# Q/k slabs as Strassen pairs, and all seven SSM projection products inside the attention stage

## The chip, the cores and the metric

The kernel runs on one core of a Trainium2 chip. The metric is device microseconds of one execution; lower is better. TensorE (PE) does the matmuls, VectorE (DVE) and ScalarE (ACT) the elementwise work, GpSimd (POOL) some masking and scaling, and SyncE (SP) issues every DMA transfer, in the order in which they stand in its program. Each of these engines works through its own list of instructions in order.

## The reference

One layer of a hybrid decoder, sequence 1024, width 1024, batch 1. A Mamba-2 (SSD) branch and an attention branch with a forget gate read the same modulated, normalised input `h`.

```python
proj = einsum("bsd,de->bse", h, w_in)                 # z, xbc, dt, q, k, v, z_att, f, gates
y_ssm = _ssd_branch(z_ssm, xbc, dt_raw, ...)          # conv, chunked state space, gated RMS norm
y_att = _fox_branch(q, k, v, z_att, f_logit, b_f)     # 8 heads of 128, causal softmax with decay
g_ssm, g_att = split(sigmoid(g_logit + b_gate), 2)
merged = g_ssm * (y_ssm @ w_proj_ssm) + g_att * (y_att @ w_proj_att)
x = x + gate * (merged @ w_out)
return _rmsnorm(x, final_norm_w)
```

Everything is float32. The kernel reaches that precision on PE by splitting each operand into a high and a low part (`split`: a CAST on ACT, a subtraction on DVE) and taking three products: high·high, high·low, low·high.

## The kernel before

The work stands in stages, one after the other in the program; a list scheduler then fixes the order on each engine, by priorities and by its own model of durations. Work that is written inside `tc.high_priority` goes first; the rest fills in where its inputs are there.

- **Input and first slabs** (to about 76 us): the modulated `h`, transposed and split, as `hh` and `hl` (8 tiles each).
- **Projection stage** (pool `pa`, to about 492 us): the columns of `w_in` are worked off as slabs of 128 output columns. `c_slab` is a plain slab: two halves of 8 x 3 matmuls of 512 columns, 48 in all. `c_pair` makes two slabs at once with Strassen's seven products (Winograd's form): 7 x 4 x 3 = 84 matmuls in place of 96, with four extra sums of weights on DVE. `PAIRS` lists the pairs, 19 of them. `w_sums`, spread over the pairs by `WPREP`, prepares the same kind of sums for the later projections.
- **State-space stage** (pool `sd`, to about 729 us): `ssd_half`, at high priority. Plain slabs fill PE beside it: three v slabs and the seven q/k slabs of `SPILL`, by the table `FILL`. A spilled slab is written to DRAM (`qk_out`).
- **Attention stage** (pools `at`, `atp`, to about 1018 us): `attend(h)` for eight heads at high priority: logits (tile `lg`), min and exp (`sm`, `pr`), scaling by POOL, transposes (`tp`), split (`pth`, `ptl`), and the product with v (`pv`). The next head's q and k come from `qk_slab`: loaded and split where they were spilled, or made on the spot by `c_slab`. `u_scaled` scales the state-space result (tile `ut`) with `rb`, a row that comes from the end of the state-space stage through DRAM, and writes `us_scr`; `PREP` says after which heads. `early` makes the SSM projection's products 1 and 2 after head 6 and product 6 after head 7. A product of a projection is four column blocks of 12 matmuls, 48 in all.
- **Last stage** (pools `frp`, `finp`): SSM products 7, 5, 4, 3, then the seven products of the attention projection (inputs `o_scr`, loaded as `b11`, `b21`, `b12`, `b22`; products 1 and 2 need `b11` and `b21`), then the seven of the output projection. Pool `frp`, which holds `b11`, `b21` and the merge tiles `m`, lies where the attention stage's pool `at` lay. `b12` and `b22` lie in pool `fin`.

The tiles `ev` (four buffers of 1024 columns) are shared by `ut`, `qt`, `vt`, `zg`, `gt` and others. DMA transfers run on eight lanes; a transfer waits for the one before it on its lane.

Of the kernel before, what the change touches and what calls it, by code (L numbers as in the profile page):

```python
# [65 lines left out]
def build(ctx, tc, t):  # L66
# [866 lines left out]
    def early(js):  # L933
# [6 lines left out]
        def form(i):  # L940
            fs = []
            for k in range(4):
                if i == 2:
                    e = piece(4 + k, LO)
                else:
                    e = piece(k, LO)
                    for q in {1: (), 6: (12, 22)}[i]:
# [10 lines left out]
        if js == (6,):  # L958
            for p in range(4):
                hi, lo = w_in("ps", 6, p)  # L960
                ps = bank()
                for k in range(4):
                    c = slice(k * P, (k + 1) * P)
                    PE.matmul(ps, lhsT=hi[:, c], rhs=fs[6][k][0], start=(k == 0), stop=False)
                    PE.matmul(ps, lhsT=hi[:, c], rhs=fs[6][k][1], start=False, stop=False)
                    PE.matmul(ps, lhsT=lo[:, c], rhs=fs[6][k][0], start=False, stop=(k == 3))
                V.tensor_tensor(out=sx[p], in0=ps, in1=sx[p], op=ALU.add)
            return
        for p in range(4):
            mine = {}  # L970
            for i in js:
                prod_c(i, "ps", fs[i], sx, mine, done, p)

    with tc.tile_pool(name="at", bufs=1, side="right") as at, \
            tc.tile_pool(name="atp", bufs=1, space=PSUM) as atp:

        def qk_slab(h):
            qh, ql, kh, kl = (at.tile([P, S], F32R, tag=n, bufs=2, name=n) for n in ("qh", "ql", "kh", "kl"))
            def q_evac(hs, ps):
                A.activation(out=qh[:, hs], in_=ps, func=AF.Copy, scale=-QSCALE)  # L980
                V.scalar_tensor_tensor(out=ql[:, hs], in0=ps, scalar=-QSCALE, in1=f32(qh[:, hs]),
                                       op0=ALU.mult, op1=ALU.subtract)

            def k_evac(hs, ps):
                A.copy(out=kh[:, hs], in_=ps)
                V.tensor_tensor(out=kl[:, hs], in0=ps, in1=f32(kh[:, hs]), op=ALU.subtract)
            for n, slab, evac, hi, lo in (("q", Q0 + h, q_evac, qh, ql), ("k", K0 + h, k_evac, kh, kl)):
# [84 lines left out]
        for h in range(AH):  # L1072
            if h == HCLOSE:
                hctx.close()
                fin = finx.enter_context(tc.tile_pool(name="fin", bufs=1))
# [19 lines left out]
    with tc.tile_pool(name="finp", bufs=1, space=PSUM) as fpp_:  # L1095
        fpp.append(fpp_)


        done_early = sum(EARLY.values(), ())
        b = {**ub, **b_quads(us_scr, (11, 21))}  # L1100
        def ssm_done(ch, tk, p, ps):
            V.scalar_tensor_tensor(out=mq[11 + 10 * ch + tk][p], in0=g_in(p + 4 * ch, tk), scalar=1.0, in1=ps,
                                   op0=ALU.add, op1=ALU.mult)
        prep_u = True
        for i in ORDER:
# [144 lines left out]
```

## Time and profile before

| | us |
|---|---|
| median of 3 runs (lowest, highest) | 1225.61 (1225.07, 1229.4) |
| the profiled execution, its own time | 1224.89 |
| span of the profile, first to last instruction | 1223.2 |
| PE, DVE, ACT, POOL busy | 1162.6, 957.2, 626.5, 88.3 |

Busy time of PE is the union of pipelined matmuls, so a PE that is always busy may still be fed too slowly; the count of matmuls in a stretch tells more. A page of the profile gives the busy time of each engine in a stretch with the number of instructions behind it (x304 is 304 instructions).

### The profile page before, as it was taken

The numbers are of one execution on the slowest core, as the hardware profiler recorded it, in microseconds if no ns is written. First come the engines' busy times: TensorE is split into PE (matmuls) and PEld (weight loads), VectorE is DVE, ScalarE is ACT, GpSimd is POOL, SyncE is SP. The second block draws the span as 40 slices with busy tenths as digits, with TensorE's granted clock in tenths as the row PEclk, the third lists the DMA queues.
The fourth block names the chain that finished last, engine by engine and source line by source line (L and its number), as shares of the span: only waits on it lengthen the run. The fifth ranks groups of instructions, "written<-read, shape, count | busy, mean of one in ns | idle before, by whom it ended". The sixth has DMA issues, their size and how long they took to land.

```text
span 1223.2 us, 18391 instructions
## 1 busy us (share of the span) xinstructions
PE 1162.6 (95%) x6206; PEld 976.3 (80%) x6206; DVE 957.2 (78%) x1950; ACT 626.5 (51%) x1252; POOL 88.3 (7%) x152
## 2 busy tenths in 40 slices
PE   4899999999999999999999989999989998999997
PEld 2788888788877878998987777888877886788876
DVE  6956689788987685589999986664677968989967
ACT  5554444453443334777676633454456644354465
POOL 2000000000000000000000002222322220000001
PEclk9899999999999999999999999999999999999999
DMA  8765543655485665646545658422255526965333
GB/s 351 274 233 184 185 154 93 231 189 189 129 309 167 224 224 200 202 152 223 187 150 186 199 213 294 155 92 73 87 176 195 182 77 239 326 190 182 104 96 147
DMA packets 109018, 228.26 MB, mean 187 GB/s; under 512 B 12362, under 2 KB 20220, under 8 KB 107900
## 3 DMA queue, kind: packets, MB, share of 16 engines
q1 hardware_dynamic: 108924, 227.09, 55.1%
q8 instruction: 49, 0.80, 0.3%
q14 instruction: 45, 0.37, 0.1%
HBM read 159.14 MB, written 67.90 MB: 186 GB/s over the span
## 4 chain that ended last, share of the span: by engine, by line
PE 66%; DVE 15%; DMA 12%; issue 4%; ACT 3%; POOL 1%; SPq 0%; DVEq 0%; POOLq 0%; ACTq 0%
PE pp L497 4%; PE pp L499 4%; PE pp L500 4%; PE pv L1061 4%; PE mm L497 3%; PE mm L499 3%; PE mm L112 3%; PE mm L500 3%; PE mm L113 3%; PE lg L1030 3%; PE mm L111 3%; DMA ab<-a_scr 3%; PE tp L1051 2%; PE mm L915 2%; PE mm L913 2%
## 5 line engine op out<-in xcount | busy, mean ns | idle before, releaser
L98 ACT CAST wh<-wr 128x512 fp32r<-128x512 f32 (+1 forms) x214 | 130.8, 619 | 171.7 <-DMA wr<-w_c 35.0
L99 DVE TENSOR_TENSOR wl<-wr,wh 128x512 fp32r<-128x512 f32 (+1 forms) x214 | 145.5, 686 | 44.9 <-ACT wh L98 44.6
L112 PE MATMUL mm<-hl,wh 128*128 128x512 f32 x288 | 116.4, 404 | 1.9 <-DVE hl L306 1.9
L111 PE MATMUL mm<-hh,wh 128*128 128x512 f32 x288 | 115.7, 406 | 0.1
L113 PE MATMUL mm<-hh,wl 128*128 128x512 f32 x288 | 115.1, 400 | 0.0
L136 PE MATMUL mm<-wh,hh 128*128 128x256 f32 (+1 forms) x256 | 73.8, 289 | 2.4 <-DVE tmp L348 2.4
L137 PE MATMUL mm<-wl,hh 128*128 128x256 f32 (+1 forms) x256 | 74.4, 292 | 0.0
L138 PE MATMUL mm<-wh,hl 128*128 128x256 f32 (+1 forms) x256 | 73.6, 288 | 0.0
L1036 ACT ACTIVATE pr<-pr,sm 128x1024 f32<-128x1024 f32 (+3 forms) x64 | 49.9, 780 | 44.8 <-DVE sm L1035 38.1
L1054 ACT CAST pth<-tp 128x512 fp32r<-128x512 f32 (+1 forms) x80 | 42.5, 542 | 53.5 <-PE tp L1051 43.7
L1031 DVE CUSTOM_DVE_ANT_0 pr<-lg,fb 128x512 f32<-128x512 f32 (+1 forms) x96 | 51.3, 551 | 18.7 <-PE lg L1030 13.2
L112 PEld LDWEIGHTS mm<-hl,wh 128*128 128x128 f32 x288 | 55.0, 191 | 13.2 <-DVE hl L306 3.3
L113 PEld LDWEIGHTS mm<-hh,wl 128*128 128x128 f32 x288 | 54.9, 191 | 10.3
L111 PEld LDWEIGHTS mm<-hh,wh 128*128 128x128 f32 x288 | 54.5, 191 | 10.5 <-ACT hh L305 0.7
L690 ACT ACTIVATE ab<-ab,acs 128x128 f32<-128x128 f32 x128 | 41.2, 391 | 37.7 <-DMA ab<-a_scr 34.1
L1055 DVE TENSOR_TENSOR ptl<-tp,pth 128x512 fp32r<-128x512 f32 (+1 forms) x80 | 49.9, 630 | 10.2 <-ACT pth L1054 9.8
L1039 POOL TENSOR_SCALAR pr<-pr,sm 128x1024 f32<-128x1024 f32 (+3 forms) x64 | 52.2, 816 | 78.2 <-DVE sm L1038 65.4
L98 ACT CAST sh<-sr 128x512 fp32r<-128x512 f32 x57 | 33.9, 619 | 42.3 <-DVE sr L479 31.3
L796 POOL TENSOR_TENSOR fl<-fl,mhalf 128x8 f32<-128x8 f32 x1 | 1.6, 1648 | 699.0 <-DVE fl L794 699.0
L136 PEld LDWEIGHTS mm<-wh,hh 128*128 128x128 f32 x256 | 48.8, 191 | 2.8 <-DVE tmp L348 2.6
L138 PEld LDWEIGHTS mm<-wh,hl 128*128 128x128 f32 x256 | 49.1, 192 | 0.0
L137 PEld LDWEIGHTS mm<-wl,hh 128*128 128x128 f32 x256 | 48.9, 191 | 0.2
(406 smaller groups left out, 3485.5 us busy)
## 6 DMA issues: line engine op xcount, KB each, us to landing
wr<-w_c SPq DMA_DIRECT2D x116, 256.0 KB, 3.7
wa<-w_ada SPq DMA_DIRECT2D x8, 1024.0 KB, 11.4
g_scr<-gt SPq DMA_DIRECT2D x16, 512.0 KB, 4.2
ab<-a_scr SPq DMA_DIRECT2D x32, 256.0 KB, 3.9
gt<-g_scr SPq DMA_DIRECT2D x32, 256.0 KB, 4.0
wr<-w_ps SPq DMA_DIRECT2D x28, 256.0 KB, 2.7
wr<-w_pa SPq DMA_DIRECT2D x28, 256.0 KB, 2.7
wr<-so SPq DMA_DIRECT2D x28, 256.0 KB, 2.7
```

Source lines behind the costliest of these rows:

```text
L98: A.copy(out=hi[:, :n], in_=raw[:, :n])
L99: eng.tensor_tensor(out=lo[:, :n], in0=raw[:, :n], in1=f32(hi[:, :n]), op=ALU.subtract)
L111: PE.matmul(ps, lhsT=hi[:, cs], rhs=xh[k][:, hs], start=(k == 0), stop=False)
L112: PE.matmul(ps, lhsT=hi[:, cs], rhs=xl[k][:, hs], start=False, stop=False)
L113: PE.matmul(ps, lhsT=lo[:, cs], rhs=xh[k][:, hs], start=False, stop=(k == 7))
L136: PE.matmul(o, lhsT=xh[k][:, ts], rhs=hi[:, cs], start=(k == 0), stop=False)
L137: PE.matmul(o, lhsT=xh[k][:, ts], rhs=lo[:, cs], start=False, stop=False)
L138: PE.matmul(o, lhsT=xl[k][:, ts], rhs=hi[:, cs], start=False, stop=(k == 7))
L497: PE.matmul(ps, lhsT=f[0][:, w], rhs=xh[:, hs], start=(first and k == 0), stop=False, skip_group_check=True)
L499: PE.matmul(ps, lhsT=f[0][:, w], rhs=xl[:, hs], start=False, stop=False, skip_group_check=True)
L500: PE.matmul(ps, lhsT=f[1][:, w], rhs=xh[:, hs], start=False, stop=(k == 3), skip_group_check=True)
L1039: G.tensor_scalar(out=pr[:, :n], in0=pr[:, :n], scalar1=sm[:, 1:2], scalar2=0.5, op0=ALU.mult, op1=ALU.mult)
```

## The change

`PSPILL` now names eight q/k slabs, which become four more entries of `PAIRS` in the projection stage (23 pairs) and are written to DRAM. `SPILL` gains k of head 7, with a place in `FILL` in the last quarter of the state-space stage. No q/k slab is left to the attention stage: `qk_slab` only loads and splits. `early` becomes `ssm_products`, which makes all seven SSM products beside the attention: 1 and 2 after head 1, 6 and 7 after head 3, 5 and 3 after head 5, 4 after head 6 (`SSM`). Every finished block is gated and written to `m_scr`, and the last stage loads all sixteen blocks back into `m`. Since `hh` and `hl` are no longer read there, their pool closes before the attention and `fin` opens in its place.

```diff
-SPILL = (("q", 0), ("k", 0), ("k", 2), ("k", 4), ("q", 7), ("k", 5), ("k", 6), )
-PSPILL = ()
+SPILL = (("q", 0), ("k", 0), ("k", 2), ("k", 4), ("q", 7), ("k", 5), ("k", 6), ("k", 7))
+PSPILL = (("q", 1), ("k", 1), ("q", 2), ("q", 3), ("k", 3), ("q", 4), ("q", 5), ("q", 6))
-HCLOSE = 6
-EARLY = {6: (1, 2), 7: (6,)}
+SSM = {1: (1, 2), 3: (6, 7), 5: (5, 3), 6: (4,)}
-PREP = (6, 1, 0, 0, 0, 0, 0, 0, 1)
+PREP = (7, 0, 0, 0, 0, 0, 0, 0, 1)
-FILL = [[], [0, 2], [4, 5, 9], [1, 3, 6, 7, 8]]
+FILL = [[], [0, 2], [4, 5, 9], [1, 3, 6, 7, 8, 10]]
...
-    def early(js):
+    def ssm_products(js):
...
+                elif i == 3:
+                    e = ub[22][k]
+                elif i == 7:
+                    e = raw_tile()[:, :512]
+                    V.tensor_tensor(out=e, in0=ub[22][k], in1=ub[12][k], op=ALU.subtract)
...
+                    if i == 4:
+                        e2 = piece(4 + k, LO)
+                        V.tensor_tensor(out=e, in0=e2, in1=e, op=ALU.subtract)
                 fs.append(b_split(e))
...
+        for p in range(4):
+            ps = mm_tile()
+            for i in js:
+                hi, lo = w_in("ps", i, p)
                 for k in range(4):
...
+                if i == 1:
+                    sx[p] = fin_tile("x1", 4)
+                    A.copy(out=sx[p], in_=ps)
+                elif i == 6:
+                    V.tensor_tensor(out=ps, in0=ps, in1=sx[p], op=ALU.add)
+                    A.copy(out=sx[p], in_=ps)
...
+                else:
+                    done(*RESULT[i], p, ps)
+
+    hctx.close()
+    fin = finx.enter_context(tc.tile_pool(name="fin", bufs=1))
...
-                if (n, h) in SPILL + PSPILL:
-                    qt = ev("qt")
-                    SP.dma_start(out=qt[:, :S], in_=qk_scr[n, h])
-                    split(qt, hi, lo, S)
-                else:
-                    c_slab(t["w_c"], slab, hh, hl, evac)
+                qt = ev("qt")
+                SP.dma_start(out=qt[:, :S], in_=qk_scr[n, h])
+                split(qt, hi, lo, S)
...
-            if h in EARLY:
-                early(EARLY[h])
-                if 1 in EARLY[h]:
+            if h in SSM:
+                ssm_products(SSM[h])
+                if 1 in SSM[h]:
                     ub = b_quads(us_scr, (12, 22))
...
-        for i in ORDER:
-            if i in done_early:
-                continue
...
-            prod_c(i, "ps", b_form(i, b, lambda: raw_tile()[:, :512]), sx, held, ssm_done)
```

The scheduler lays the instructions out anew. Three places show how.

DVE in head 0 of the attention. Before, the scaled `ut` tiles stand among the head's own work (`pr`, `sm`, `ptl`) and the split of weights (`wl`) of the slabs that are made there:

```order
L813 SCALAR_TENSOR_TENSOR ut<-ut,cols,rb 128x1024
L1035 TENSOR_TENSOR sm<-sm 128x1
L1038 RECIPROCAL sm<-sm 128x1
L1055 TENSOR_TENSOR ptl<-tp,pth 128x512
L813 SCALAR_TENSOR_TENSOR ut<-ut,cols,rb 128x1024
L1055 TENSOR_TENSOR ptl<-tp,pth 128x512
L1031 ISA pr,sm<-lg,fb 128x512
```

Now the same place holds, besides `ut`, the split `bl` of SSM product 1's input, whose `wr` is loaded from the `us_scr` just written:

```order
L812 SCALAR_TENSOR_TENSOR ut<-ut,cols,rb 128x1024
L1068 TENSOR_TENSOR ptl<-tp,pth 128x512
L1051 RECIPROCAL sm<-sm 128x1
L812 SCALAR_TENSOR_TENSOR ut<-ut,cols,rb 128x1024
L1068 TENSOR_TENSOR ptl<-tp,pth 128x512
L98 TENSOR_TENSOR bl<-wr,bh 128x512
L1044 ISA pr,sm<-lg,fb 128x512
```

All eight `ut` operations stand inside head 0 in both. The eight `bl` of products 1 and 2 now stand within heads 0 and 1, and on SP sixteen re-loads of `us_scr` (eight for these `bl`, eight for `b12` and `b22`) between and behind the stores of `ut`; before, these `bl` and re-loads stood in heads 4 and 5.

SP at the end of the attention. Before, the store of the last head is followed by the inputs of the SSM products (`us_scr`) and then by those of the attention projection:

```order
L1065 DMA o_scr_94<-zg 128x1024
L920 DMA b_11141<-us_scr_173 128x512
L920 DMA b_11143<-us_scr_174 128x512
L920 DMA b_11145<-us_scr_175 128x512
L920 DMA b_11147<-us_scr_176 128x512
L920 DMA b_11149<-us_scr_177 128x512
L920 DMA b_11151<-us_scr_178 128x512
L928 DMA gt<-g_scr_102 128x512
L920 DMA b_11597<-o_scr_87 128x512
```

Now fourteen of the sixteen loads of `m` stand between that store and the first `b11`:

```order
L1078 DMA o_scr_94<-zg 128x1024
L1109 DMA m<-m_scr_9242 128x512
...
L1109 DMA m<-m_scr_11404 128x512
L1109 DMA m<-m_scr_11429 128x512
L919 DMA b_11758<-o_scr_87 128x512
L919 DMA b_11760<-o_scr_88 128x512
```

PE at the same place. Before, the last `pv` is followed by the rest of SSM product 7, whose input lies in pool `fin`:

```order
L1061 MATMUL pv<-pth,vh 128x128
L1061 MATMUL pv<-pth,vl 128x128
L1061 MATMUL pv<-ptl,vh 128x128
L913 MATMUL pp<-bh,wh 128x512
L914 MATMUL pp<-bl,wh 128x512
```

Now product 1 of the attention projection follows, whose `bh` and `bl` are made from `b11`:

```order
L1074 MATMUL pv<-pth,vh 128x128
L1074 MATMUL pv<-pth,vl 128x128
L1074 MATMUL pv<-ptl,vh 128x128
L912 MATMUL mm<-bh,wh 128x512 x3
L912 MATMUL pp<-bh,wh 128x512
```

PE's program has 6175 matmuls before and 6127 now. Of the 336 matmuls of the SSM products, 14 stand in head 1 of the attention, 151 in head 2, 63 in the first half of head 3, 36 and 48 in the halves of head 5, and 24 in the first half of head 6; heads 0, 4 and 7 have none.

More of the change, by code (lines that the diff above doesn't have):

```diff
@@ L978, in qk_slab @@
             qh, ql, kh, kl = (at.tile([P, S], F32R, tag=n, bufs=2, name=n) for n in ("qh", "ql", "kh", "kl"))
[L979 to L987, printed above, removed]
-                if (n, h) in SPILL + PSPILL:
-                    qt = ev("qt")
-                    SP.dma_start(out=qt[:, :S], in_=qk_scr[n, h])
-                    split(qt, hi, lo, S)
-                else:
-                    c_slab(t["w_c"], slab, hh, hl, evac)
+            for n, hi, lo in (("q", qh, ql), ("k", kh, kl)):
+                qt = ev("qt")
+                SP.dma_start(out=qt[:, :S], in_=qk_scr[n, h])
+                split(qt, hi, lo, S)
             return qh, ql, kh, kl
@@ L1096, in build @@
         fpp.append(fpp_)
[L1099 to L1104, printed above, removed]
-        for i in ORDER:
-            if i in done_early:
-                continue
-            if i in (5, 4) and prep_u:
-                prep_u = False
-                for p in range(4):
-                    t2 = tt_tile()
-                    V.tensor_tensor(out=b[11][p], in0=b[12][p], in1=b[11][p], op=ALU.subtract)
-                    V.tensor_tensor(out=t2, in0=b[22][p], in1=b[11][p], op=ALU.subtract)
-                    V.tensor_tensor(out=b[21][p], in0=b[21][p], in1=t2, op=ALU.subtract)
-            prod_c(i, "ps", b_form(i, b, lambda: raw_tile()[:, :512]), sx, held, ssm_done)
         for ch, tk, p in m_scr:
```

33 lines of the change are left out of this document (16 added, 17 removed).

## Prediction

> **What bounds the kernel now.** I read the page's busy times and chain first, then busy times by stage, then the counts of matmuls in each stage, then single stretches of the attention. The page (busy time, share, instructions; then the chain that ended last):
>
> ```profile
> PE 1162.6 (95%) x6206; PEld 976.3 (80%) x6206; DVE 957.2 (78%) x1950; ACT 626.5 (51%) x1252; POOL 88.3 (7%) x152
> PE 66%; DVE 15%; DMA 12%; issue 4%; ACT 3%; POOL 1%; SPq 0%; DVEq 0%; POOLq 0%; ACTq 0%
> ```
>
> PE carries the chain, so the first question is what a matmul costs when nothing holds it up. A stretch of the last stage (start:end, length, then busy time and count for PE, weight load, DVE, ACT, POOL, then clock, DMA share, GB/s), and the stages in the same columns:
>
> ```profile
> 1080.00:1150.00 70.00, 70.00 (x304) 56.91 (x304) 62.93 (x104) 35.68 (x63) 0.00 (x0) 1.00 0.53 164
> 76.00:492.00 416.00, 409.02 (x1836) 334.31 (x1835) 324.59 (x514) 179.61 (x316) 0.00 (x0) 1.00 0.58 197
> 492.00:729.00 237.00, 227.51 (x1692) 204.42 (x1690) 207.32 (x495) 160.22 (x386) 1.65 (x1) 1.00 0.57 183
> 729.00:1018.00 289.00, 276.59 (x1596) 239.19 (x1596) 197.29 (x509) 143.02 (x291) 75.46 (x128) 0.98 0.44 148
> 1018.00:1223.20 205.20, 193.51 (x828) 154.97 (x828) 176.36 (x302) 104.20 (x197) 4.69 (x8) 0.99 0.58 191
> ```
>
> A 512-column matmul costs 70/304 = 0.2303 us. The last stage has 828 of them: 190.7 us of 205.2. So the projection and last stages are paid for by the matmul. How many of the others are fill shows by source line; each line stands for a third of its matmuls (PE and weight load only: projection pairs; plain slabs in the state-space stage and in the attention; SSM products in the attention, on two lines):
>
> ```profile
> 76.00:492.00 416.00, 208.80 (x532) 100.01 (x532) 1.00 0.58 197
> 492.00:729.00 237.00, 54.43 (x136) 25.64 (x136) 1.00 0.57 183
> 729.00:1018.00 289.00, 47.72 (x120) 22.72 (x120) 0.98 0.44 148
> 729.00:1018.00 289.00, 17.48 (x44) 8.30 (x44) 0.98 0.44 148
> 729.00:1018.00 289.00, 6.38 (x16) 3.00 (x16) 0.98 0.44 148
> ```
>
> Pairs: 3 x 532 = 1596 = 19 x 84. Plain slabs in the state-space stage: 408, so half a slab more than the seven of SPILL already sits there. Attention: 3 x (120 + 44 + 16) = 540 fill matmuls. Now the attention by stretch; heads 0, halves of heads 1 and 3 and 4 without any fill, heads 5 and 6 with the SSM products, head 7:
>
> ```profile
> 729.10:788.90 59.80, 56.86 (x294) 47.67 (x294) 39.47 (x88) 22.40 (x44) 13.82 (x22) 0.98 0.70 244
> 788.90:798.40 9.50, 9.50 (x77) 9.07 (x76) 7.64 (x26) 6.98 (x16) 4.20 (x9) 1.00 0.31 111
> 857.70:867.20 9.50, 9.50 (x77) 9.07 (x76) 7.63 (x28) 6.93 (x16) 4.13 (x9) 1.00 0.33 112
> 886.60:897.90 11.30, 10.24 (x76) 9.21 (x75) 8.75 (x27) 8.02 (x17) 4.11 (x9) 1.00 0.38 139
> 913.20:997.50 84.30, 79.48 (x440) 68.33 (x440) 66.49 (x158) 48.04 (x95) 20.60 (x31) 0.96 0.53 170
> 997.50:1017.60 20.10, 17.50 (x124) 15.22 (x122) 12.63 (x42) 10.60 (x24) 6.59 (x13) 1.00 0.14 51
> ```
>
> Half a head without fill takes 9.5 us. Sixteen of those and 540 x 0.2303 make 152 + 124.4 = 276.4; the stretch from first to last attention matmul (729.1 to 1017.6) took 288.5, so 12.1 are lost, most of them in head 0 and where the SSM inputs come.
>
> **The change part by part.** The order of the changed program gives the counts (6175 matmuls become 6127).
>
> Projection stage: four pairs more, 336 matmuls x 0.2303 = 77.4. The stage as a whole has 416 us for what is mostly dense, 7 of them idle, so 77.4 x 416/409 = 78.7; I take +78.5 (77.4 to 82). DVE is 78% busy there, and the new pairs need no silu or convolution, so it covers their sums.
>
> State-space stage: 408 fill matmuls become 384, -24 x 0.2303 = -5.5 if PE sets it. PE is idle for 9.5 of 237 and DVE 87% busy; some of the 5.5 will stay: -4. The first logits waited for a transfer that now stands earlier on SP (second row):
>
> ```profile
> 727.31 0.27 PE L798 MATMUL sp<-ident,fl 128*8 128x128 f32 x1 [1.99 <-POOL fl L796]
> 729.09 0.77 PE L1030 MATMUL lg<-kh,qh 128*128 128x512 f32 x1 [1.50 <-DMA fb<-f_scr]
> ```
>
> That gives -1; together -5 (-7 to 0).
>
> Attention, DVE: it does 121 operations of 512 columns beside the heads' own where it did 85, and 29 of 1024 where it did 20 (all q/k splits, seven products' inputs, weights, evacuations). Back to back they cost (from the chain and DVE's list; the brackets give idle time and its cause):
>
> ```profile
> 1029.38 1.88 DVE bl L99 x3
> 738.40 2.48 DVE L813 SCALAR_TENSOR_TENSOR ut<-ut,cols,rb 128x1024 f32<-128x1024 f32 x2 [2.51 <-DMA rb<-r_scr]
> 754.71 1.28 DVE L813 SCALAR_TENSOR_TENSOR ut<-ut,cols,rb 128x1024 f32<-128x1024 f32 x1 [1.34 <-DMA ut<-u_scr]
> 758.04 1.27 DVE L813 SCALAR_TENSOR_TENSOR ut<-ut,cols,rb 128x1024 f32<-128x1024 f32 x1
> ```
>
> So 36 x 0.63 + 9 x 1.24 = 33.9 more: DVE goes from 197.3 to 231. That is the floor of the new attention. PE's own floor is 152 + 336 x 0.2303 = 229.4. Two engines within 2 us of each other, coupled link by link, won't both be full. By stretches:
>
> - Heads 0 and 1, 14 fill matmuls. DVE takes its operations in order, and the eight ut among head 0's own wait for DMA, as the rows above do. The row at 738.40 starts 9.3 after the first logits, the seventh ends at 759.3, or +30.2. Now an eighth comes in head 0 (+3.3, the mean step of these), and eight 256-KB re-loads stand on SP ahead of it, four more than the weight loads they replace; at the 0.74 each of the burst shown below that is +3 to +6. Head 0 so ends at +37 to +43, with PE mostly waiting. Head 1 then needs two halves of 7.64 on DVE and ten splits: 21, less some logits done early. I take 60 (55 to 65), where before 14 fill matmuls would have cost 41.
> - Head 2 and half of head 3: 3 x 9.5 + 214 x 0.2303 = 77.8. The row 913.20 had the same mix: 38 + 180 x 0.2303 = 79.5 took 84.3, a factor 1.06: 82.5.
> - To the end of head 4: 3 x 9.5, one at 11.3: 30.5.
> - Head 5 and half of head 6: (28.5 + 108 x 0.2303) x 1.06 = 56.6.
> - The rest: 9.5 + 20.1 = 29.6.
>
> Sum 259, so -29.5 against 288.5. Ends: 241 (229.4 and the old loss), 272 (DVE 85% busy).
>
> Last stage: 828 matmuls become 672, -156 x 0.2303 = -35.9. But its start changes. Before, PE ran on into product 7 (first row), and the burst of loads had cover. Now product 1 of the attention projection needs b11, behind the last head's store and fourteen loads of m on SP:
>
> ```profile
> 1018.37 0.50 PE L913 MATMUL pp<-bh,wh 128*128 128x512 f32 x1 [0.52 <-DVE zg L1064]
> 1018.81 0.38 SPq L1065 DMA_DIRECT2D o_scr<-zg  x1
> 1027.76 5.94 SPq L920 DMA_DIRECT2D b<-o_scr  x8
> 1030.00:1034.00 4.00, 3.89 (x17) 3.20 (x18) 4.00 (x8) 1.47 (x3) 0.00 (x0) 1.00 1.04 386
> 1018.40:1042.00 23.60, 20.83 (x84) 15.55 (x85) 21.15 (x35) 10.09 (x18) 0.00 (x0) 1.00 1.00 349
> L98 ACT CAST bh<-b 128x512 fp32r<-128x512 f32 x32 | 19.0, 619 | 11.3 <-DVE b L1112 6.8 <-DVE b L1114 3.0 <-PE pp L913 0.6
> ```
>
> The store went out 1.2 after the last pv (1017.6). In the burst a 256-KB load takes 5.94/8 = 0.74, with DMA full at 386 GB/s; the 512-KB store and fifteen loads take 1.5 + 11.1; the cast 0.62. First matmul at +14.4 instead of +0.8: +13.6 (+5, if the loads of m could overlap the tail of head 7, to +18). In exchange the 23.6 us of the row 1018.40, in which 84 matmuls are 19.3 of work, no longer lose 4.3. A long idle PE then starts slowly, as it did at the first logits:
>
> ```profile
> 725.40:728.60 3.20, 0.27 (x1) 0.08 (x1) 2.29 (x3) 3.20 (x4) 1.65 (x1) 1.00 0.39 150
> 728.60:732.00 3.40, 2.91 (x7) 2.36 (x8) 3.40 (x7) 1.16 (x3) 0.60 (x2) 0.50 1.01 400
> ```
>
> 3.4 us at a granted clock of 0.50 cost 1.7. Last stage: -35.9 + 13.6 - 4.3 + 1.7 = -24.9.
>
> Sum: +78.5 - 5 - 29.5 - 24.9 = +19.1. The profiled execution took 1224.89 (span 1223.2 and 1.7 around it), 0.7 under the median of 1225.61: 1244.0.
>
> **The rivals.**
>
> Work alone decides (faster). PE is busy 95% and the matmuls are fewer: -48 x 0.2303 = -11.1, 1213.9. For it: four of five stages run near 0.23 per matmul, and half heads without fill keep PE at 9.50 of 9.50. Against it: DVE's 231. It holds if attention falls by all 204 matmuls, 47.0 to 241.5, and the gap before the last stage stays hidden; each us over 241.5 or of gap takes one away, and from 11 us on nothing is gained.
>
> Half of it (no change). The prefetched q, k and v let head 0 run through, attention takes 246, and the gap stays: 78.5 - 5 - 42.5 - 24.9 = +6, 1231.
>
> A cold PE in the attention (slower still). In the row 725.40 PE had next to nothing to do for 3.2 us, and in the next row it ran at 0.50 for 3.4 us, which costs 1.7. With less fill there are more such gaps, in head 0 above all, where I have PE waiting for some 20 us in several pieces; DVE, near its limit, then waits for PE in turn. Eight such gaps cost 13.6 and bring the attention to the 272 that DVE at 85% would take as well: 1257. Against it: the half heads without fill kept a clock of 1.00 and the whole attention 0.98.
>
> The Trainium skill, page "TensorE: Matmul & The Clock Gate", section "HAM oscillation — how this bites in real kernels", has this as a rule: no idle gap of PE over about 3.4 us, or it starts cold each time. By that rule each of the waits for DMA in head 0 would add its own cold start, as in this rival; the trace has one such case beside it, 0.50 for 3.4 us, and shows no series of them.
>
> **How the numbers follow.** Forecast (1232 to 1252) 0.57, cold PE 0.13, no change 0.18, work alone 0.12. Half a per cent, 6 us, is what a measurement of this kernel tells from nothing. Slower 0.70, same 0.18, faster 0.12. The range for 8 in 10 leaves out most of the work-alone case and of the cold PE: 1220 to 1259; the forecast's own is 1232 to 1252.
>
> **What would show it.** In the changed profile: the last pair ends near 570 and the first logits start near 803 (a later start than 808 refutes the state-space term). Head 0 ends 37 to 43 us later, with DVE idle before ut for DMA. From first logits to last pv 259, DVE busy some 231 of it. Then PE idle for 14 us, SP issuing loads of m, the clock at 0.50 behind it, and 166 us more of last stage. If attention comes out under 245 my view of DVE is wrong; if the gap is under 8 us, that of the queue.

## The result, and the profile after

The changed kernel takes 1272.07 us (median of 4, 1270.79 to 1275.34) against 1226.82 for the kernel before (4 runs): a ratio of 1.038 (1.0362 to 1.0399). The forecast was 1244, with 1220 to 1259 as the range for 8 in 10. The direction was right, the size was not: the loss is 45 us where 19 were forecast.

The profiled execution took 1275.34 (span 1273.6) and is the slowest of the four. The page, busy time and the chain that ended last:

```profile
PE 1172.8 (92%) x6158; PEld 982.2 (77%) x6158; DVE 985.0 (77%) x1985; ACT 650.8 (51%) x1289; POOL 94.1 (7%) x152
PE 58%; DVE 17%; DMA 14%; ACT 5%; issue 4%; SPq 1%; POOL 1%; DVEq 0%; POOLq 0%; ACTq 0%
```

PE has 8 points less of the chain, shared out over DVE, DMA and ACT: no single engine took its place. The stages (columns as in the prediction): projection, its new end, state-space stage; then the attention by the prediction's stretches, the gap, and the last stage from its first matmul:

```profile
76.00:492.00 416.00, 409.58 (x1839) 335.40 (x1839) 330.59 (x524) 180.68 (x321) 0.00 (x0) 1.00 0.58 196
492.00:570.00 78.00, 78.00 (x345) 63.74 (x344) 30.64 (x47) 29.83 (x52) 0.00 (x0) 1.00 0.36 121
570.00:801.00 231.00, 220.32 (x1658) 199.20 (x1656) 203.70 (x490) 157.55 (x381) 1.65 (x1) 0.99 0.54 177
...
801.00:870.40 69.40, 52.95 (x283) 43.82 (x284) 55.90 (x130) 37.39 (x73) 21.42 (x34) 0.83 0.89 316
870.40:953.20 82.80, 79.97 (x432) 67.74 (x431) 68.00 (x150) 50.15 (x96) 21.14 (x28) 1.00 0.59 192
953.20:996.20 43.00, 34.41 (x192) 29.22 (x191) 34.83 (x89) 21.15 (x41) 12.45 (x21) 0.84 0.50 160
996.20:1059.90 63.70, 56.39 (x320) 48.14 (x319) 49.44 (x123) 30.19 (x60) 17.34 (x28) 0.97 0.63 207
1059.90:1089.50 29.60, 26.86 (x175) 23.53 (x173) 18.68 (x63) 14.66 (x34) 8.78 (x17) 0.94 0.26 90
1089.50:1106.40 16.90, 0.01 (x1) 0.01 (x1) 0.45 (x2) 0.68 (x2) 0.00 (x0) 0.53 0.95 335
1106.40:1273.60 167.20, 158.12 (x672) 127.79 (x672) 140.93 (x243) 89.06 (x170) 4.68 (x8) 0.97 0.48 157
```

| stretch | forecast | measured | miss |
|---|---|---|---|
| start of the first logits | 802.6 | 801.0 | -1.6 |
| heads 0 and 1 | 60 | 69.4 | +9.4 |
| head 2 and half of 3 | 82.5 | 82.8 | +0.3 |
| to the end of head 4 | 30.5 | 43.0 | +12.5 |
| head 5 and half of 6 | 56.6 | 63.7 | +7.1 |
| the rest | 29.6 | 29.6 | 0.0 |
| last stage | 180.7 | 184.1 | +3.4 |

These add up to the 31 us between the forecast span of 1242.3 and 1273.6. The attention did not get shorter at all: 288.5 us to the end of its last pv, 288.8 before, with 204 matmuls fewer. Its PE is busy in 79.97 of 82.80 where the products stand, and in 34.41 of 43.00 where they don't.

The last stage starts late as forecast. SP (start, duration, line, transfer) and PE (in brackets the idle time and its cause):

```profile
1090.84 9.03 SPq L1109 DMA_DIRECT2D m<-m_scr  x14
1100.21 5.74 SPq L919 DMA_DIRECT2D b<-o_scr  x9
```

```profile
1089.18 0.28 PE L1074 MATMUL pv<-ptl,vh 128*128 128x128 f32 x1
1106.39 1.65 PE L912 MATMUL mm<-bh,wh 128*128 128x512 f32 x3 [16.93 <-ACT bh L97]
```

Fourteen loads of m go out ahead of b11, and PE stands for 16.9 us (the forecast had the first matmul 14.4 after the last pv).

### The profile page after: what moved, and what is told of

It is laid out like the page before. It is cut to its first block, busy times and chain, and to the rows that moved or that the text cites. A ratio compares the mean times of both kernels' runs of the same rounds, so it can differ in the third digit from the quotient of the medians.

```text
span 1273.6 us, 18429 instructions
## 1 busy us (share of the span) xinstructions
PE 1172.8 (92%) x6158; PEld 982.2 (77%) x6158; DVE 985.0 (77%) x1985; ACT 650.8 (51%) x1289; POOL 94.1 (7%) x152
## 4 chain that ended last, share of the span: by engine, by line
PE 58%; DVE 17%; DMA 14%; ACT 5%; issue 4%; SPq 1%; POOL 1%; DVEq 0%; POOLq 0%; ACTq 0%
PE pp L496 6%; PE pp L498 6%; PE pp L499 6%; PE mm L496 4%; PE mm L499 4%; PE mm L498 4%; DMA ab<-a_scr 3%; PE pv L1074 2%; PE lg L1043 2%; DMA wr<-us_scr 1%; PE pp L1163 1%; PE tp L1064 1%; PE pp L1165 1%; PE pp L1166 1%; DVE pr L1044 1%
## 5 line engine op out<-in xcount | busy, mean ns | idle before, releaser
L97 ACT CAST sh<-sr 128x512 fp32r<-128x512 f32 x69 | 41.4, 619 | 57.8 <-DVE sr L478 34.7
L111 PE MATMUL mm<-hl,wh 128*128 128x512 f32 x160 | 65.5, 410 | 1.6 <-DVE hl L305 1.6
L112 PE MATMUL mm<-hh,wl 128*128 128x512 f32 x160 | 64.5, 404 | 0.0
L110 PE MATMUL mm<-hh,wh 128*128 128x512 f32 x160 | 63.9, 408 | 0.4 <-ACT hh L304 0.4
L1074 PE MATMUL pv<-ptl,vh 128*128 128x256 f32 (+1 forms) x160 | 50.8, 318 | 8.1 <-DVE ptl L1068 8.0
L689 ACT ACTIVATE ab<-ab,acs 128x128 f32<-128x128 f32 x128 | 41.1, 391 | 33.1 <-DMA ab<-a_scr 30.4
L98 DVE TENSOR_TENSOR sl<-sr,sh 128x512 fp32r<-128x512 f32 x69 | 46.1, 685 | 13.7 <-PE pp L499 7.8
L1043 PE MATMUL lg<-kh,qh 128*128 128x512 f32 (+1 forms) x96 | 39.4, 412 | 15.1 <-DVE sm L1044 13.3
L1074 PE MATMUL pv<-pth,vh 128*128 128x256 f32 (+1 forms) x160 | 47.9, 299 | 5.6 <-DVE zg L1077 2.6
L972 PE MATMUL mm<-bh,wh 128*128 128x512 f32 x112 | 46.0, 411 | 6.3 <-DVE mm L987 2.7
L1064 PE MATMUL tp<-ident,pr 128*128 128x128 f32 x288 | 46.9, 291 | 4.6 <-POOL pr L1052 4.3
## 6 DMA issues: line engine op xcount, KB each, us to landing
wa<-w_ada SPq DMA_DIRECT2D x8, 1024.0 KB, 11.4
```

Of the source, the lines that this page charges most:

```text
L97: A.copy(out=hi[:, :n], in_=raw[:, :n])
L98: eng.tensor_tensor(out=lo[:, :n], in0=raw[:, :n], in1=f32(hi[:, :n]), op=ALU.subtract)
L111: PE.matmul(ps, lhsT=hi[:, cs], rhs=xl[k][:, hs], start=False, stop=False)
L1043: PE.matmul(lg[:, :n1 - n0], lhsT=x[:, bs], rhs=y[:, n0:n1], start=(i == 0), stop=(i == 2))
L1074: PE.matmul(pv[:, o0:256], lhsT=x[kb // 4][:, kb % 4, vs], rhs=y[:, d:d + m], start=(kb == 0 and i == 0), stop=(kb == 2 * qq + 1 and i == 2))
```

## The experiments

Layouts differ in when the first logits start, by up to 13 us, so the attention is compared by its own length, from the first logits to the end of the last pv. Its fill is the count of its matmuls less 1056, the heads' own. A half head ends with the 30th or the 60th of a head's 60 pv matmuls. The times given are medians; the rows come from one profiled execution of each run.

**The queue of loads.** In the last stage, the loads of m were put behind b11:

```diff
-        for ch, tk, p in m_scr:
-            SP.dma_start(out=mq[...][p], in_=m_scr[ch, tk, p])
         b = b_quads(o_scr, (11, 21, 12, 22))
+        for ch, tk, p in m_scr:
+            SP.dma_start(out=mq[...][p], in_=m_scr[ch, tk, p])
```

> The sixteen loads of the merge tiles m are written behind the loads of the attention projection's inputs (b11, b21, ...) instead of ahead of them; nothing else changes. Theory Q (the gap of 17.2 us between the last pv and the first matmul of the last stage is the queue of m loads ahead of b11): the gap falls to 6 to 9 us, since the fourteen loads took about 9.8 us of it, and the time from 1272 to 1261-1265. Rival R (the burst of loads as a whole is limited by the transfers' rate): PE starts earlier but waits the same sum a little later, at product 6 or at the first merged tile; the time stays at 1269-1273.

1263.54 us. The stretches of this run, attention, gap, rest:

```profile
801.40:1084.20 282.80, 246.19 (x1392) 207.81 (x1392) 227.80 (x550) 154.08 (x302) 80.46 (x128) 0.95 0.64 214
1084.20:1088.20 4.00, 0.02 (x1) 0.00 (x0) 0.43 (x2) 0.62 (x1) 0.00 (x0) 0.68 0.68 218
1088.20:1255.70 167.50, 158.17 (x672) 127.44 (x672) 141.30 (x243) 89.16 (x170) 4.68 (x8) 0.98 0.55 185
```

The gap is 4.0 in place of 16.9 (6 to 9 expected), and what follows takes the same time (167.50, 167.20): nothing waits later. Q holds. Another 5.7 us of this profile lie in the attention, whose program is the same and whose clock was better (0.95, against 0.92 as the mean of the five stretches above). The profiled execution is the fastest of its five (1257.5), and the medians differ by 8.5 us only, so this attention of 282.8 is likely on the short side.

**Three causes in the attention.** Extra matmuls that keep PE warm; no low parts; no re-loads. Their edits, the main lines:

```diff
+            for _ in range({0: 6, 1: 2, 5: 4, 7: 2}.get(h, 0)):      # warm: 12 matmuls each
+                wps = mm_tile()
+                for i in range(12):
+                    PE.matmul(wps, lhsT=qnow[0][:, :P], rhs=qnow[2][:, :512], start=(i == 0), stop=(i == 11))
```

```diff
-                fs.append(b_split(e))                                # no low parts: inputs
+                hi = fin_tile("bh", 8, F32R)
+                A.copy(out=hi, in_=e)
+                fs.append((hi, hi))
...
-                hi, lo = w_in("ps", i, p)                            # and weights
+                raw = raw_tile()
+                SP.dma_start(out=raw[:, :512], in_=w_src("ps", i, p))
+                hi = lo = hi_tile()
+                A.copy(out=hi[:, :512], in_=raw[:, :512])
```

```diff
-            SP.dma_start(out=e, in_=us_scr[j][:, hs])                # no re-loads
+            A.copy(out=e, in_=rb[:, hs])
...
-                    ub = b_quads(us_scr, (12, 22))
+                    ub = {q: [loaded(f"b{q}", None) for _ in range(4)] for q in (12, 22)}
```

In the last one `loaded` with None copies a part of `rb` too.

> 168 extra matmuls of 512 columns, whose results are not used, are added as low-priority fill: 74 stand in head 0, 48 in head 4, 24 in head 6. They are 38.7 us more of PE work (168 x 0.2303) and, since the scheduler lays the products out anew around them, products 1 to 7 are spread a little more evenly. Theory K (the half clock in the gaps of PE is what lengthens the attention: 44 us at half clock in it): the clock stays near 1.00 in the attention, which ends in 268 to 278 us in place of 288 although PE has more to do; the time is 1252-1262. Theories V (DVE's own work and order set the attention) and D (the transfers do): the attention stays at 285 to 300, the time at 1269-1285.

> The low parts of the inputs and weights of the seven SSM products are left out: the subtraction on DVE is gone (56 operations of 512 columns, 38.6 us of DVE time as the attention's rows have them), and the matmuls that used the low part use the high part again, so that PE has the same count. Theory V (DVE's work is the bound of the attention): the attention falls by 25 to 38 us, to 250-263, and the time to 1234-1247. Theories K (cold clock) and D (transfers): 0 to 8 us, all of it outside heads 0 and 1, the time 1264-1272.

> The 32 loads from us_scr (8.4 MB of the attention's 60 MB) are left out: the SSM products take a copy of a row block that is already in SBUF as their input; the stores to us_scr stay, and so does every matmul. Theory D (transfers, and the wait for the scaled ut to come back, hold heads 0 and 1 up, where DMA was 0.89 to 0.90 busy): heads 0 and 1 together fall from 69.4 to 50-58 us with the same or more matmuls in them, and the time to 1254-1262. Theory K alone: heads 0 and 1 fall too, but only because products now stand in head 0 and keep the clock up; heads 3.5 to 5, which stay without fill, keep their 43 us. Theory V: heads 0 and 1 stay within 4 us of 69.4.

They took 1292.96, 1272.26 and 1275.31 us. The attention of each, in that order:

```profile
810.30:1106.50 296.20, 272.05 (x1539) 230.70 (x1537) 225.78 (x549) 152.73 (x301) 81.11 (x126) 0.98 0.59 197
```

```profile
806.20:1087.80 281.60, 245.44 (x1392) 207.87 (x1392) 197.26 (x494) 153.40 (x302) 76.57 (x128) 0.95 0.63 215
```

```profile
802.80:1091.20 288.40, 248.25 (x1392) 210.04 (x1392) 228.85 (x550) 170.23 (x334) 80.50 (x128) 0.92 0.54 181
```

All three theories fell in the form they had. With the clock at 0.98 the attention is longer, not shorter (the time lies above both expectations, since the first logits also start 9.3 us later; why wasn't tried). With DVE 30 us less busy it gains 6.9 us, not 25. Without 32 loads it gains nothing; there 72 of the products' matmuls moved into head 0, which then took 70.0 us in place of 46.7, and later heads became shorter by as much. That run isn't a clean test of the transfers, since 32 copies on ACT stand in for the loads (170.23 us busy, 153.54 before that edit). One number pointed on: the 147 extra matmuls of the warm run are 33.9 us of work and cost 7.7. Of the 26 us in between, the better clock may be up to 16 (0.92 of 288.5 us leaves 22 us short of full speed, 0.98 of 296.2 leaves 6); the rest says that the changed kernel's heads have room that the products don't use.

**What the heads cost alone.** The products are left out (`SSM = {}`), with the merge tiles loaded from elsewhere and behind b11; then u_scaled as well (`PREP` all 0).

> The seven SSM products of the attention stage are left out, with their inputs, weights and stores (336 matmuls, 77.4 us of PE work); the merge tiles are loaded from us_scr instead, behind b11. Theory L (the products' operations and loads stand in the in-order queues ahead of the heads' own and stall them): the attention without them takes 165 to 185 us (19 per head, some 20 to 30 more for head 0), so that in the changed kernel they cost 103 to 123 us for 77.4 of work. Rival B (the heads themselves are slower in this layout, whatever stands beside them): 205 to 215, so the products cost no more than their work. Theory K (clock): without fill the heads leave so many gaps that the clock falls to half over most of the stage, and it takes over 215.

> As the run without the products, and the eight u_scaled steps are left out too (their loads, the DVE operation, the stores); the merge tiles are loaded from u_scr. Theory H (head 0 is held up by the u_scaled chain: load, DVE in order, store): the first head and a half falls from some 50 us to 30 to 36, and the attention by 15 to 22 us against the run without the products. Rival: heads 0 and 1 are held up by the loads of q, k, v, f, whatever u_scaled does: less than 8 us.

1187.88 and 1176.37 us. Without products, the attention, the same by the stretches of the table above, and the two halves of head 3:

```profile
808.30:1013.40 205.10, 171.88 (x1056) 144.48 (x1056) 155.12 (x429) 115.14 (x229) 73.22 (x128) 0.93 0.48 164
...
808.30:879.00 70.70, 53.37 (x281) 44.74 (x282) 54.08 (x131) 34.57 (x64) 23.78 (x37) 0.79 0.72 247
879.00:914.60 35.60, 31.09 (x206) 26.20 (x205) 26.13 (x79) 22.41 (x46) 13.88 (x26) 1.00 0.42 148
914.60:948.30 33.70, 29.38 (x192) 24.69 (x191) 28.18 (x80) 21.24 (x42) 10.92 (x22) 1.00 0.48 155
948.30:984.80 36.50, 32.38 (x209) 26.50 (x208) 27.18 (x82) 22.13 (x45) 15.62 (x27) 1.00 0.37 125
984.80:1013.40 28.60, 25.67 (x178) 22.35 (x176) 19.55 (x63) 14.79 (x34) 9.03 (x18) 1.00 0.10 37
...
901.30:914.60 13.30, 11.68 (x77) 9.47 (x76) 8.79 (x29) 8.09 (x17) 6.47 (x11) 1.00 0.30 116
914.60:925.40 10.80, 9.61 (x63) 8.06 (x62) 10.45 (x29) 6.45 (x13) 3.41 (x7) 1.00 0.56 161
```

Without ut too:

```profile
809.20:1000.70 191.50, 167.69 (x1056) 140.87 (x1056) 145.29 (x421) 113.65 (x229) 72.37 (x128) 0.97 0.39 131
```

Theory L fell and B held: 205.1, not 165 to 185. The heads alone take 191.5 us without ut, of which head 0 has 32.9; heads 1 to 5 (842.1 to 960.0, 117.9 us) take 11.8 a half. PE isn't what bounds such a half: the 77 matmuls of the row 901.30 take 13.3 us here, and 78 take 9.50 in the run with even slabs below. What is left is the chain of logits, min, exp, scaling, transposes and split. The prediction's 9.5 belongs to another case. The ut chain adds 13.6 (15 to 22 expected), 11.4 of it in head 0: H is right in kind, a little large. The products of the changed kernel cost 288.5 - 205.1 = 83.4 us (77.7 with b11 first) for 77.4 of work: in sum nothing of them is hidden.

**Spread out.** b11 first, and

```diff
-SSM = {1: (1, 2), 3: (6, 7), 5: (5, 3), 6: (4,)}
+SSM = {3: (1, 2), 4: (6, 7), 5: (5, 3), 6: (4,)}
-PREP = (7, 0, 0, 0, 0, 0, 0, 0, 1)
+PREP = (2, 3, 2, 0, 0, 0, 0, 0, 1)
```

> b11 first, and the tables changed: u_scaled 3, 3, 2 in heads 0, 1, 2 and the products behind heads 3, 4, 5 and 6, so that 49, 47, 63, 64, 17, 23, 37, 36 matmuls stand in the half heads 3.0 to 6.5 in place of 119 in one half and none in head 4. Theory L in its first form (bursts of products and empty heads cost; spread out they fit): the attention falls from 283-288 to 260-272, the time from 1263.5 to 1240-1251. Rival (each product costs its coupling wherever it stands): 280-288, the time 1260-1268.

> The spread tables with b11 first, and the low parts of the products' inputs and weights left out (56 operations of DVE less, the matmuls use the high part twice). Theory V2 (a product's DVE operations delay the heads' chain, which the run without low parts alone could not show because its matmuls stood in bursts with PE full): the attention falls from 284.7 to 250-262, the time from 1263.6 to 1229-1241. Rival: it is the loads and the order, not DVE's operations: 275 or more, the time 1254 or more.

1263.57 us and, with the low parts left out too, 1256.51. The attention of each:

```profile
802.20:1086.90 284.70, 247.93 (x1392) 208.41 (x1392) 227.77 (x550) 153.26 (x302) 85.08 (x128) 0.94 0.63 212
```

```profile
804.40:1083.80 279.40, 247.35 (x1392) 212.66 (x1392) 193.61 (x494) 153.64 (x302) 82.59 (x128) 0.92 0.65 216
```

Both rivals held: neither spreading over heads 3 to 6 nor DVE's low parts is the answer.

**PE's part and the rest.** Extra matmuls without inputs of their own (as in the warm run, 12 for each unit of the table) in the kernel without products, spread from head 0 on (`{0: 4, 1: 4, 2: 4, 3: 4, 4: 4, 5: 4, 6: 2, 7: 2}`) or late (`{3: 6, 4: 10, 5: 6, 6: 6}`, with u_scaled spread as in the spread run); and the products with two matmuls for each block of weights in place of twelve, b11 first, then also without the low parts:

```diff
-                for k in range(4):
-                    ...
+                PE.matmul(ps, lhsT=hi[:, :P], rhs=fs[i][0][0], start=(i == js[0]), stop=False, ...)
+                PE.matmul(ps, lhsT=lo[:, :P], rhs=fs[i][0][1], start=False, stop=True, ...)
```

> The kernel without the products, and 336 extra matmuls of 512 columns whose inputs lie ready and whose results are not used, 314 of them beside the heads (74 in head 0, 12 to 48 in most half heads up to 6.0). Theory F (the heads leave PE some 70 us that fill without inputs of its own can take): the attention grows from 205.1 to 225-245, 0.06 to 0.13 us for a matmul of 0.23. Rival P (a fill matmul costs its PE time wherever it stands, as my sum had it): 270-280.

> The kernel without the products, u_scaled spread over heads 0 to 2, and 336 extra matmuls without inputs of their own, but all of them in the seven half heads 2.5 to 5.5 (72, 22, 69, 56, 45, 24, 48), where the spread products stood in about the same way. If the place decides (a half head has some 2.5 to 4.5 us of room, and more fill than that pays its full time): the attention takes 260 to 282 in place of 237.4 with the same fill spread from head 0 on. If the inputs decide (DVE, loads): 235 to 250.

> The products keep their loads, casts, sums, splits, evacuations and stores, but make 56 matmuls in place of 336; b11 first. Theory V2 (DVE's and the loads' part of a product is what the heads pay for): the attention stays at 250-280, of 282.8 with all the matmuls. Rival P: it falls to 212-225, that is 205.1 and 56 matmuls.

> 56 matmuls in place of 336, and no low parts of the products' inputs and weights (56 operations of DVE less); b11 first. If DVE's operations are what the heads pay for when PE is not full: the attention falls from 263.9 by 25 to 38 us to 226-239. If it is the loads and the order in the queues: 252-264.

1226.65, 1242.18, 1237.57 and 1223.69 us. The attention of each, and for the first also its first half head:

```profile
814.00:1051.50 237.50, 223.97 (x1371) 196.62 (x1370) 151.93 (x428) 113.11 (x228) 70.90 (x126) 0.99 0.40 134
814.00:849.80 35.80, 32.25 (x166) 27.07 (x166) 23.41 (x50) 10.84 (x20) 7.78 (x13) 0.95 0.79 264
```

```profile
809.40:1068.90 259.50, 238.25 (x1392) 206.94 (x1392) 155.99 (x429) 114.75 (x229) 73.44 (x128) 0.94 0.38 129
```

```profile
800.60:1064.50 263.90, 203.32 (x1112) 166.03 (x1112) 225.12 (x550) 153.96 (x302) 86.74 (x128) 0.88 0.68 229
```

```profile
802.10:1050.80 248.70, 196.78 (x1112) 161.88 (x1112) 193.91 (x494) 152.96 (x302) 80.76 (x128) 0.90 0.71 242
```

F holds: plain fill costs 32.4 us for 315 matmuls, 0.10 each (the time grows by 38.8, since the first logits start 5.7 later here). In head 0 seventy-four of them (17.0 us of work) cost 3.0: the half head takes 35.8, and 32.8 with none. The fill also lifts the clock from 0.93 to 0.99, and no run separates what it hides in waits from what it gives back in this way; by these clocks the second is at most 12 us of the 40 that are not paid. The same fill late costs 54.4, 0.16 each, just under what the place theory expected. And the products with hardly any matmuls still cost 263.9 - 205.1 = 58.8, where their 56 matmuls are 12.9 of work; V2 holds here. Their clock was 0.88, though, so the cold PE may be a part of the 58.8. Taking the low parts away gives back 15.2, half of what DVE alone would, and 248.7 lies between the two expectations: the other part is loads, casts, order and the clock, which no run separates.

**Halves of the change.** The kernel before with only the Strassen pairs; and the changed kernel with two of the four pairs taken back, the products spread and b11 first (the main lines of the edits):

```diff
-SPILL = (("q", 0), ("k", 0), ("k", 2), ("k", 4), ("q", 7), ("k", 5), ("k", 6), )
+SPILL = (("q", 0), ("k", 0), ("k", 2), ("k", 4), ("q", 7), ("k", 5), ("k", 6), ("k", 7))
-PSPILL = ()
+PSPILL = (("q", 1), ("k", 1), ("q", 2), ("q", 3), ("k", 3), ("q", 4), ("q", 5), ("q", 6))
-FILL = [[], [0, 2], [4, 5, 9], [1, 3, 6, 7, 8]]
+FILL = [[], [0, 2], [4, 5, 9], [1, 3, 6, 7, 8, 10]]
```

```diff
-PSPILL = (("q", 1), ("k", 1), ("q", 2), ("q", 3), ("k", 3), ("q", 4), ("q", 5), ("q", 6))
+PSPILL = (("k", 3), ("q", 4), ("q", 5), ("q", 6))
-SSM = {1: (1, 2), 3: (6, 7), 5: (5, 3), 6: (4,)}
+SSM = {3: (1, 2), 4: (6, 7), 5: (5, 3), 6: (4,)}
```

> The kernel before with only the first half of the change: the eight q/k slabs as Strassen pairs and k of head 7 in the state-space stage. The SSM products stay as before (1, 2, 6 and a part of 7 beside the attention, 180 matmuls there or right behind it). If the SSM move alone carries the loss: first logits at 801, attention 205 to 225, last stage 205, the time 1213 to 1233. Rival (q/k slabs were good cover for the heads, and without them the attention loses whatever stands there): attention 245 or more, the time over 1252.

> Two of the four new pairs are taken back: q and k of head 1 and q of heads 2 and 3 are plain slabs again (101 of their 192 matmuls stand in head 0, the others in the state-space stage), the products stand behind heads 3, 4, 5 and 6, b11 first. Theory F (head 0, which waits for the scaled ut, takes independent fill nearly free): first logits at 778-790, the attention 285-297, the time 1242-1255 against 1263.5 with four pairs. Rival P: the attention grows by the full 23 us to 306, the time 1262-1270.

1249.62 and 1247.83 us. Pairs alone, attention and last stage:

```profile
800.90:1041.60 240.70, 209.84 (x1236) 178.19 (x1236) 191.03 (x488) 137.67 (x272) 80.49 (x128) 0.94 0.57 190
1041.60:1247.70 206.10, 193.41 (x829) 155.01 (x828) 176.33 (x302) 104.09 (x197) 4.68 (x8) 0.99 0.58 190
```

Two pairs, attention and its first half head:

```profile
779.00:1074.70 295.70, 263.77 (x1494) 223.46 (x1492) 222.55 (x551) 151.27 (x302) 77.06 (x126) 0.97 0.57 190
779.00:812.10 33.10, 31.43 (x169) 26.60 (x168) 21.02 (x49) 9.88 (x21) 6.83 (x13) 1.00 0.81 286
```

The pairs alone lose 24.5 us by the spans (1247.7 against 1223.2), between the two expectations and nearer the rival: 71.8 more before the attention, 48.1 less in it for 360 matmuls (82.9 us of work), 0.8 more behind. The rest of the loss by the spans, 25.9 (22.4 by the medians), is the move of the SSM products: the attention grows by 47.8 for 156 matmuls, and the last stage gives back 22.0. With two pairs F holds in all its numbers: 77 matmuls of plain slabs (17.7 us) stand in head 0's first half, which takes 33.1 us; with none it took 32.1.

**Back to the kernel before.** All seven products in the last stage (`EARLY = {}`); also with the last two gate pairs made plain beside heads 3 to 6 (with four entries of WPREP moved up by one or two pairs); the first with q of head 7 plain and k of head 3 spilled; and that with `EARLY = {7: (1, 2)}`.

> The kernel before with all seven SSM products in the last stage (180 matmuls go there from the attention, which keeps its 360 of the plain slabs). By the price of fill in the runs: first logits at 729, the attention 245 to 256 (205 and 360 plain ones at 0.11 to 0.14), the last stage 247 to 254 (205 and 180 x 0.23 and a gap of 4), the time 1221-1238, no clear change. Rival P: 1227 to 1233 too, by full price on both sides; the attention tells them apart, at 247 (P: 288.5 less 41.5) against 249 or more.

> As the run before, and the last two pairs of gate slabs leave the projection stage: their four slabs are made plain (192 matmuls in place of 168), one each behind heads 3, 4, 5 and 6, so that the half heads 3.0 to 6.0 hold 24 to 57 matmuls of fill each and the stage 552. Theory F (spread plain fill costs 0.10 to 0.20): first logits at 690, the attention 267 to 288, the last stage 247 to 254, the time 1206-1229, likeliest 1215. Rival P: the attention grows by the full 44 us, the time is 5 us over the run before.

> The kernel before with the SSM products in the last stage, and another choice of spilled slabs: q of head 7 is made plain beside the attention and k of head 3 spilled in its place. The 360 matmuls of fill then stand as 48 in each head up to head 5 (head 2 had 96), and 24 in head 6. If the place decides: head 2 falls by 9 to 11 us, heads 4.5 to 6 grow by 5 to 8, the attention comes to 242-245 in place of 246.8 and the time to 1222-1226 in place of 1227.7. Rival P: 246-248 and 1226-1229.

> As the run with even slabs, and products 1 and 2 (96 matmuls) beside head 6's second half and head 7, which held no fill, in place of the last stage. If the place decides: they cost 0.10 to 0.17 there in place of 0.23, the attention 252-261, the last stage 226-229, the time 1214-1223. If a product's inputs cost its full price wherever it stands: 264-268, the time 1223-1229.

The medians are 1227.70, 1246.03, 1225.74 and 1235.90 us; ratios to the kernel before 0.9994 (0.9979 to 1.0010), 1.0140 (1.0116 to 1.0164), 0.9997 (0.9984 to 1.0010) and 1.0079 (1.0063 to 1.0095). Products late, the attention:

```profile
730.40:977.20 246.80, 235.26 (x1416) 204.21 (x1416) 164.17 (x454) 122.38 (x253) 72.05 (x128) 0.99 0.40 135
```

Even slabs, the attention and four half heads in a row, with 48, 0, 48 and 0 matmuls of fill:

```profile
729.90:973.50 243.60, 234.43 (x1416) 204.28 (x1416) 164.76 (x454) 121.82 (x253) 71.64 (x128) 0.99 0.40 137
858.10:877.40 19.30, 19.30 (x108) 16.65 (x107) 12.01 (x32) 8.65 (x18) 5.04 (x8) 1.00 0.33 110
877.40:888.80 11.40, 10.35 (x78) 9.33 (x77) 8.84 (x29) 8.07 (x17) 4.14 (x9) 1.00 0.38 139
888.80:908.10 19.30, 19.30 (x108) 16.66 (x107) 10.79 (x31) 7.57 (x16) 4.11 (x8) 1.00 0.26 84
908.10:917.60 9.50, 9.50 (x78) 9.08 (x76) 7.64 (x28) 6.92 (x16) 4.13 (x9) 1.00 0.30 110
```

Gates beside the heads: projection stage, state-space stage, attention. Then products 1 and 2 beside heads 6 and 7, the attention:

```profile
76.00:466.80 390.80, 378.22 (x1716) 309.18 (x1715) 306.06 (x485) 164.28 (x288) 0.00 (x0) 0.99 0.59 201
466.80:713.10 246.30, 227.08 (x1652) 203.62 (x1652) 208.22 (x496) 159.71 (x386) 1.65 (x1) 0.97 0.55 176
...
713.10:1000.60 287.50, 279.01 (x1608) 241.54 (x1608) 172.28 (x462) 132.29 (x269) 73.73 (x128) 0.99 0.38 130
```

```profile
731.80:1002.50 270.70, 258.43 (x1512) 225.83 (x1512) 180.00 (x477) 131.77 (x272) 73.41 (x128) 0.97 0.42 142
```

Products late: the attention falls by 42.0 for 180 matmuls, the full 0.23 of each (247 expected of rival P), so the products hid nothing in the kernel before either; the time stays. Gates late was a miss: the first logits start at 713, not 690, since two pairs fewer shortened the projection stage by 25 of 38.7 us and the next stage grew by 9 (why wasn't tried), and 192 more of fill in a PE that was 95% busy cost 40.7, 0.21 each. Even slabs: 243.6 as expected, but 3 us can't be told from the kernel before. The last one decides for the inputs: two products in empty half heads cost 270.7 - 243.6 = 27.1 for 96, 0.28 each, more than either expectation had. No version that does the whole work was measurably faster than the kernel before.

What a fill matmul costs beside the heads, over their own 205.1 (its work is 0.23):

| fill | matmuls | attention | each |
|---|---|---|---|
| extra matmuls, from head 0 on | 315 | 237.5 | 0.10 |
| plain slabs, even | 360 | 243.6 | 0.11 |
| plain slabs, as before | 360 | 246.8 | 0.12 |
| extra matmuls, late | 336 | 259.5 | 0.16 |
| plain slabs and products 1, 2, 6 and a part of 7 (before) | 540 | 288.8 | 0.15 |
| products 1 to 7, b11 first | 336 | 282.8 | 0.23 |
| products 1 to 7, spread | 336 | 284.7 | 0.24 |
| products 1 to 7 (after) | 336 | 288.5 | 0.25 |

The 205.1 belongs to the changed layout. The kernel before wasn't run without its fill, so the rows with plain slabs are estimates from that number.

## Why the prediction was right in direction and wrong in size

- Projection and state-space stages: +78.5 - 5 was forecast, 71.9 came. The last pair ends at 570 and the first logits start at 801.0. Right. (408 plain matmuls are one and a half slabs more than seven, not half a slab; the step to 384 holds all the same.)
- Attention, DVE's work: 231 forecast, 226.9 measured. The number is right, but as a floor it decided nothing: 30 us less of it changed the attention by 6.9.
- **Attention, the heads' own time: a half head without fill counted as 9.5 us. This step failed.** Without its fill, which it prices at 85 us with the factor 1.06, the sum has 174 us for the heads alone; the run without products has 205.1. The table below splits every stretch in this way. Both rows of 9.50 were half heads behind one that was full of fill. The even slabs show such half heads at 9.50 and 11.40; as I read it, the other engines run ahead while PE works off the fill, and the next half finds its inputs ready (no run shows that by itself). Alone a half takes 11.8.
- Heads 0 and 1, the other part of the same step: head 0 ended at +46.7 (37 to 43 forecast). Without any product it ends at +44.3 (808.3 to 852.6 in that run), so the products' loads, which I had blamed, are 2 to 3 of it. Head 1 alone takes 26.4, where the sum had 21 with its fill. The eighth ut was no news: before, it stood in head 0 too, at 777.74.
- Attention, fill at its work x 1.06: right in sum (85 forecast, 83.4 measured) but wrong in place, so the agreement is in part luck. The 82.8 us of head 2 and half of 3, for 82.5 forecast, are luck altogether. The heads were 7 us too short there and the products 7 too dear. In turn, 9.3 of the 12.5 us missed to the end of head 4 come with the products, though none of their matmuls stand there: nine of their sums on DVE (6.2 us), loads for them, and a clock of 0.84 that is 1.00 without them. A price by the matmul can't see that.
- Before, the 180 matmuls of the products cost their full 42.0 us, and the 360 of the plain slabs 41.7 for 82.9 of work; 144 of these stood in head 0. The change replaces fill that needs only weights by fill that waits for ut and brings its own loads, casts and sums, and leaves heads 0, 4 and 7 with none.

| stretch | heads, forecast | heads, measured alone | products, forecast | products, measured as the rest |
|---|---|---|---|---|
| heads 0 and 1 | 57 | 70.7 | 3 | -1.3 |
| head 2 and half of 3 | 28.5 | 35.6 | 54 | 47.2 |
| to the end of head 4 | 30.5 | 33.7 | 0 | 9.3 |
| head 5 and half of 6 | 28.5 | 36.5 | 28 | 27.2 |
| the rest | 29.6 | 28.6 | 0 | 1.0 |
| sum | 174 | 205.1 | 85 | 83.4 |

- Last stage: the gap was 16.9 (14.4), the burst and the half clock behind it as described: 184.1 against 180.7. Putting b11 first removed 12.9 of the gap. Right.
- The rivals: the cold PE came nearest (1257, chance 0.13). Its 8 gaps x 1.7 us are 13.6; the trace has some 45 us at half clock in the attention (worked out from the clocks of its five stretches), which is 22 us short of full speed. The warm run, 7.7 us longer at a clock of 0.98, shows that the clock alone is not the cause; what part it has stays open. Before, there was a second case besides the one that the prediction names: 0.50 for 6.8 us from 916.3 on.

## What to carry to other kernels

Price fill by what it adds to a stage that runs without it, not by its own work: measure the stage empty first, and don't take a short stretch beside a full one for its empty length. In these runs fill that needed nothing but weights was cheap beside a chain of engines, the more so when it was spread, and work that brings loads, casts and sums paid its full time there and did as well in a dense stage. Its cost shows up where its sums and loads stand, not only where its matmuls do. Fewer matmuls are no gain where those removed were hidden.

## What the runs showed of the hardware

The half clock needs no long gap. PE of the changed kernel, in stretches of 3.4 us and what followed (length, PE busy and count, clock, DMA share, GB/s):

```profile
954.07:957.49 3.42, 1.42 (x10) 1.00 0.51 153
957.49:964.32 6.83, 5.56 (x20) 0.50 0.81 252
...
1056.47:1059.89 3.42, 1.41 (x12) 1.00 0.75 230
1059.89:1063.30 3.41, 3.41 (x15) 0.50 0.80 244
```

Both times PE was busy for 41% of 3.42 us, in pieces, and the next stretch ran at 0.50. The longest single wait of PE within the attention:

```profile
809.43 0.79 PE L1043 MATMUL lg<-kh,qh 128*128 128x512 f32 x1 [3.17 <-DVE sm L1044]
```

The Trainium skill, page "TensorE: Matmul & The Clock Gate", section "HAM oscillation — how this bites in real kernels", puts the rule as no idle gap over about 3.4 us. No wait in the attention was that long, and the clock still fell; here it followed the busy share of a stretch of 3.4 us. The half heads without fill, with PE busy for 11.68 of 13.30 us, kept a clock of 1.00. Cut from one change of the clock on into stretches of 3.41 us, the twenty profiles have 99 stretches at a clock of 1.00 in which PE was busy for under 47% of the time, and each was followed by 0.50; of the 119 with 47 to 70% 24 were, and of the 5168 with more none.
